# Loading a neighbourhood head's values: four copies of 32 rows in place of one copy over four groups of rows

## The chip, the cores and the metric

The kernel runs on one core of one Trainium2 chip. The metric is the device time of one execution in microseconds. The time before is the median of three runs; a profile of one further execution is read beside it. "PE" is the matrix engine, "DVE", "ACT" and "POOL" are the vector, scalar and general engines, and "SP" is the engine that here issues every DMA. A DMA copy is carried by up to 16 DMA engines side by side.

## What is computed

One layer of a hybrid trunk over 1024 latent tokens on a grid 64 wide (16 rows of 64) and 256 context tokens, all in float32: a half-step SwiGLU, then two token mixers on one normalised input (neighbourhood attention and latent attention, eight heads each), merged by gates, then a second half-step SwiGLU. The change lies in the neighbourhood attention. There, each block of 16 query columns reads keys and values from 32 neighbouring columns:

```
def row(r):
    rs = jnp.clip(r - kh // 2, 0, n_rows - kh)
    ...
    k_b = jnp.moveaxis(lax.dynamic_slice_in_dim(kg, rs, kh, axis=1)[:, :, key_col], 2, 1)
    v_b = jnp.moveaxis(lax.dynamic_slice_in_dim(vg, rs, kh, axis=1)[:, :, key_col], 2, 1)
    ...
    p = jax.nn.softmax(jnp.concatenate([s_loc, s_ctx], axis=-1), axis=-1).astype(v.dtype)
    o = (jnp.einsum('bhjqak,bjakhd->bjqhd', p_loc, v_b)
         + jnp.einsum('bhjqk,bkhd->bjqhd', p[..., n_loc:], v_ctx))
```

`key_col` gives, for column block j, the 32 columns from 0, 8, 24 or 32 on.

## The kernel before

The program runs in stages: first SwiGLU, the input projections, the attention stage, the merge, the second SwiGLU. The projections write queries, keys and values to DRAM scratch tensors (`qas`, `kas`, `vws` and others), and the attention stage reads them back head by head.

The attention stage works through a list `todo` of 64 items: items 0 to 31 are the eight neighbourhood heads with four column blocks each (`NaItem`, j = 0 to 3), items 32 to 63 are the eight latent-attention heads (`MlaItem`). An item has scores (matmuls into PSUM, the bias added on DVE, a softmax on ACT) and values (transposes, splits into a high and a low part, matmuls with the value tile, `weigh`). The scores of an item are computed three items ahead of its values (`AHEAD = 3`). `head_out` ends an item; its line 1777 runs once for each item and is used below as the mark of an item.

When the first item of a neighbourhood head is started, `NaHead.loads` issues all of that head's loads, in this order: `q` and `ql` (512 KB each), the context keys `kvc` (128 KB), the keys `k` (512 KB), the bias of block 0 (384 KB), the values `va` of blocks 0 and 1, the context values (128 KB), the bias of blocks 1 and 2, the values `vb` of blocks 2 and 3, the bias of block 3. A value tile (`va`, `vb`) holds two column blocks side by side, 512 KB. In `vws` a head's values are 256 rows of 512 floats: row r * 64 + x holds column x, and the four groups r are copied to partitions 32 r to 32 r + 31 of the tile. One column block is a quarter of the head's values, 256 KB, and is loaded by one call of `values`, which issued one DMA.

The weight tiles `W` come from a pool of 16 buffers, eight of which a head takes, so the loads of a head wait for tiles of earlier heads. `ld` goes through `put`, line 132, which issues on SP; every load and store in the program therefore has line 132. SP takes its DMAs in the order of the program. The framework gives the DMAs eight completion semaphores in turn (DMAHW0 to DMAHW7 in the rows below), so that each DMA waits until the one eight places before it has landed. PE's order in the attention stage is that of the program; instructions on DVE, ACT and POOL that are not pinned are ordered by the framework's scheduler.

Of the kernel before, what the change touches and what calls it, by code (L numbers as in the profile page):

```python
# [33 lines left out]
KSTART = (0, 8, 24, 32)  # L34
# [4 lines left out]
def f32(ap):  # L39
    return ap.bitcast(F32)  # L40
# [3 lines left out]
def hybrid_block(ctx: ExitStack, tc: tile.TileContext, a: dict, out: bass.AP):  # L44
# [37 lines left out]
    def DR(shape):  # L82
        n = nm("d")
        return dp.tile(shape, F32, tag=n, name=n)
# [37 lines left out]
    def ld(dst, src):  # L122
        for x in [x for x in waiting if x[1].tensor.name == src.tensor.name]:
            waiting.remove(x)
            put(*x[1:])
        return put(dst, src)
# [4 lines left out]
    def put(dst, src):  # L131
        return pin(nc.sync.dma_start(dst, src))  # L132
# [949 lines left out]
    o = len(plan.main)  # L1082
# [93 lines left out]
    o = d1_at + 4 * NP  # L1176
# [9 lines left out]
    for f, x in ups:  # L1186
        o = len(plan.main)
# [5 lines left out]
    for e in range(2):  # L1193
        for f in range(NF):
            o = len(plan.main)
# [70 lines left out]
    def emit_cq(i, ci, x, bank):  # L1266

        t, q = x, T2()
        if bank:
            t = T2()  # L1270
            act.copy(t, x)
        act.activation(q, t, AF.Square)
        if ci in sq:
            vec.tensor_tensor(sq[ci], sq[ci], q, op=ALU.add)
        else:
            sq[ci] = q
        store(cqx[i, :, ci * 512:(ci + 1) * 512], t)
# [22 lines left out]
    for p in range(3):  # L1300
        punits.append(Unit(h2, [cq_src(2 * p), cq_src(2 * p + 1)],
                           lambda i, ci, x, bank, p=p: emit_cq(2 * p + i, ci, x, bank)))

    o = len(plan.main)
# [46 lines left out]
    vws = DR([NH, 2 * P, 512])  # L1351
# [126 lines left out]
    o = len(plan.main)  # L1478
# [98 lines left out]
    class NaHead:  # L1577
# [46 lines left out]

        def values(self, v, j):
            o = (j % 2) * 512
            ld(f32(v[:, o:o + 512]), vws[self.h].rearrange("(r x) c -> r x c", r=4)[:, KSTART[j]:KSTART[j] + 32, :])

    def na_loads(h):
        heads["na", h] = x = NaHead()  # L1630
# [96 lines left out]
    o = c_at  # L1727
# [9 lines left out]
    o = len(plan.main)  # L1737
# [3 lines left out]
    o = len(plan.main)  # L1741
# [3 lines left out]
    o = len(plan.main)  # L1745
# [4 lines left out]
    o = len(plan.main)  # L1750
# [417 lines left out]
    for d in range(KD):  # L2168
        o = len(plan.main)
# [37 lines left out]
    o = len(plan.main)  # L2207
# [13 lines left out]
    o = len(plan.main)  # L2221
# [67 lines left out]
    for j in range(4):  # L2289
        o = d2_at + 5 * NP + 2 * j  # L2290
        for x, i in enumerate((-2, 0, 1)):
            plan.spread([lambda j=j, x=x: done2(j, x)], o + i, o + i + 1)
        o = e - 9 + j
        plan.spread([lambda j=j: done_half(4 + j, 1)], o, o + 1)
        o = e - 4 + j
# [83 lines left out]
```

## Time and profile before

| what | value |
|---|---|
| time before, median of 3 runs | 2599.38 us (2599.0 to 2601.32) |
| the profiled execution's own time | 2602.28 us |
| its span in the profile | 2600.5 us |
| mean granted clock of PE | 0.991 |
| PE busy | 2538.6 us, 98% |
| DVE busy | 1962.0 us, 75% |
| ACT busy | 1276.7 us, 49% |
| DMA | 471.74 MB, mean 181 GB/s |

Busy shares are means over stages that differ. The 40 slices of the page are 65 us each; the neighbourhood heads lie in slices 21 to 24, from about 1340 to 1535 us. A row of the windows view gives, for one stretch, each engine's busy time and instruction count, then PE's granted clock, the mean busy share of the 16 DMA engines, and the GB/s moved. Shares a little over 1 occur because packets overlap at their ends. A row of the view of one line gives the shortest, median and longest duration, and the first and last start. "SPq" is SP's DMA queue: its durations are those of issuing a DMA, not of its transfer.

### The profile page before, as it was taken

To read this page: it belongs to the slowest core of one execution; us is meant where nothing else is said; L and a number is where in the kernel's file an instruction comes from. 1 tells how busy PE (TensorE), PEld (TensorE's weight loads), DVE (VectorE), ACT (ScalarE), POOL (GpSimd) and SP (SyncE) were. 2 spreads that over 40 slices of the span, in tenths; PEclk is the share of its full clock that TensorE was granted. 3 is DMA by queue.
4 is the path that set the end of the run, shared out by engine and by line. 5 is a ranking of instruction groups with operands and counts; after the bars stand their busy time and mean duration, and the time that the engine had idled before them with its cause. 6 is when DMAs were issued, how large, how long until landed. Compare 5 with 4: busy or idle time off the path is not lost.

```text
span 2600.5 us, 38171 instructions
## 1 busy us (share of the span) xinstructions
PE 2538.6 (98%) x13368; PEld 2171.9 (84%) x13368; DVE 1962.0 (75%) x3671; ACT 1276.7 (49%) x2417; POOL 235.7 (9%) x388
## 2 busy tenths in 40 slices
PE   8999999999999999999988899999999999999998
PEld 6888888888998888889877789998888888888887
DVE  4788986797675578867756788887886888767777
ACT  6623224446654743435546777785167422333444
POOL 1000000001100000003003322221011000000003
PEclk9999999999999999999998999999999999999999
DMA  8555543943765556845866653214846444336824
GB/s 306 166 174 192 181 161 127 328 134 125 261 233 164 210 210 202 280 131 171 297 223 191 186 122 76 76 31 152 330 166 221 154 160 157 115 103 220 284 73 162
DMA packets 236289, 471.74 MB, mean 181 GB/s; under 512 B 30208, under 2 KB 63680, under 8 KB 236096
## 3 DMA queue, kind: packets, MB, share of 16 engines
q1 hardware_dynamic: 236096, 469.29, 54.3%
q8 instruction: 106, 1.74, 0.3%
q14 instruction: 87, 0.71, 0.1%
HBM read 348.80 MB, written 120.39 MB: 180 GB/s over the span
## 4 chain that ended last, share of the span: by engine, by line
PE 80%; DVE 6%; ACT 6%; DMA 5%; issue 3%; SPq 1%; POOL 0%; DVEq 0%; POOLq 0%; ACTq 0%
PE bs L154 34%; PE bm L154 25%; PE bv L154 18%; ACT xu L1936 2%; DVE xu L1800 2%; DMA w<-in_bias 1%; DVE t L1963 1%; ACT t L1962 1%; PE bm L157 1%; DMA xy<-in_bias 1%; DVE xu L120 1%; DVE xv L120 1%; ACT t L120 1%; SPq L132 1%; DMA w<-d 1%
## 5 line engine op out<-in xcount | busy, mean ns | idle before, releaser
L120 ACT CAST xu<-t 128x512 fp32r<-128x512 f32 (+1 forms) x270 | 160.9, 601 | 494.0 <-DVE t L120 352.4
L154 PE MATMUL bm<-xu,xu 128*128 128x512 f32 (+1 forms) x1500 | 356.6, 391 | 0.1
L154 PE MATMUL bs<-xv,xu 128*128 128x512 f32 (+1 forms) x1452 | 347.6, 388 | 0.6 <-DVE xv L120 0.3
L154 PE MATMUL bv<-xv,xu 128*128 128x512 f32 x1342 | 335.5, 389 | 0.0
L154 PEld LDWEIGHTS bm<-xu,xu 128*128 128x128 f32 x1500 | 278.2, 188 | 57.0 <-DVE t L120 0.5
L154 PEld LDWEIGHTS bs<-xv,xu 128*128 128x128 f32 x1452 | 272.0, 188 | 56.8 <-issue 1.1
L154 PEld LDWEIGHTS bv<-xv,xu 128*128 128x128 f32 x1342 | 251.8, 188 | 52.2
L154 PE MATMUL bs<-xv,xv 128*128 128x512 f32 (+1 forms) x1134 | 274.6, 387 | 0.0
L120 DVE TENSOR_TENSOR xu<-xu,xu 128x512 fp32r<-128x512 f32 (+2 forms) x300 | 203.9, 683 | 60.6 <-ACT xu L120 60.5
L154 PEld LDWEIGHTS bs<-xv,xv 128*128 128x128 f32 x1134 | 211.3, 188 | 40.8
L154 PE MATMUL bs<-w,w 96*128 96x512 f32 (+3 forms) x832 | 214.6, 377 | 28.7 <-DMA w<-d 15.1
L120 DVE TENSOR_TENSOR t<-t,t 128x512 f32<-128x512 f32 (+2 forms) x278 | 185.0, 672 | 43.2 <-ACT t L120 34.2
L154 PE MATMUL bs<-xu,xu 128*128 128x512 f32 x900 | 216.0, 388 | 0.0
L120 POOL TENSOR_SCALAR st<-st 128x1 f32<-128x1 f32 (+1 forms) x66 | 35.8, 542 | 1918.8 <-ACT t L120 1621.6
L154 PEld LDWEIGHTS bs<-xu,xu 128*128 128x128 f32 x900 | 167.7, 188 | 35.7 <-issue 1.4
L120 ACT CAST xv<-t 128x512 fp32r<-128x512 f32 x170 | 105.8, 622 | 166.1 <-PE bm L154 69.5
L120 DVE TENSOR_TENSOR xu<-t,xu 128x512 fp32r<-128x512 f32 (+1 forms) x270 | 179.0, 663 | 10.7 <-ACT xu L120 10.6
L154 PE MATMUL bm<-xv,xv 128*128 128x512 f32 (+1 forms) x690 | 182.7, 388 | 0.0
L120 ACT CAST xu<-xu 128x512 fp32r<-128x512 f32 (+1 forms) x226 | 133.7, 603 | 72.6 <-DMA xu<-in_wo 50.9
L120 DVE TENSOR_TENSOR xv<-t,xv 128x512 fp32r<-128x512 f32 x170 | 116.6, 686 | 65.3 <-ACT xv L120 64.9
L154 PEld LDWEIGHTS bs<-w,w 96*128 96x128 f32 (+1 forms) x832 | 128.9, 198 | 40.7 <-DVE st L1825 12.3
L154 PE MATMUL bv<-t,w 128*128 128x256 f32 x896 | 153.7, 293 | 7.5 <-issue 5.9
(250 smaller groups left out, 4352.0 us busy)
## 6 DMA issues: line engine op xcount, KB each, us to landing
d<-t SPq DMA_DIRECT2D x358, 256.0 KB, 2.5
t<-d SPq DMA_DIRECT2D x274, 256.0 KB, 3.8
xu<-in_f1w SPq DMA_DIRECT2D x59, 512.0 KB, 4.1
xu<-in_f2w SPq DMA_DIRECT2D x58, 512.0 KB, 3.6
t<-in_wada SPq DMA_DIRECT2D x112, 256.0 KB, 5.5
xv<-in_f1w SPq DMA_DIRECT2D x44, 512.0 KB, 8.2
xu<-in_winT SPq DMA_DIRECT2D x34, 512.0 KB, 4.8
w<-d SPq DMA_DIRECT2D x32, 512.0 KB, 13.9
```

The costliest lines, as they stand in the source:

```text
L120: return lambda *x, **y: pin(f(*x, **y))
L132: return pin(nc.sync.dma_start(dst, src))
L154: return pin(nc.tensor.matmul(o, s, m, start=start, stop=stop, skip_group_check=open_group[0]))
L157: return pin(nc.tensor.transpose(o, x, i))
L1800: nc.vector.tensor_scalar(dst, src, 1.0, FMIN, op0=ALU.mult, op1=ALU.max, accum_out=m)
L1936: nc.scalar.activation(x, x, AF.Exp, bias=n_[:, s:s + 1], accum_out=l[:, i:i + 1])
L1962: nc.scalar.copy(t[0], pb)
L1963: nc.vector.tensor_tensor(t[1], pb, f32(t[0]), op=ALU.subtract)
```

## The change

```diff
         def values(self, v, j):
             o = (j % 2) * 512
-            ld(f32(v[:, o:o + 512]), vws[self.h].rearrange("(r x) c -> r x c", r=4)[:, KSTART[j]:KSTART[j] + 32, :])
+            for r in range(4):
+                x = r * 64 + KSTART[j]
+                ld(f32(v[r * 32:r * 32 + 32, o:o + 512]), vws[self.h, x:x + 32, :])
```

The same bytes go to the same places. Each of the 32 loads of a column block's values becomes four loads of 64 KB, so the program issues 96 DMAs more. Lines after 1627 move down by two.

On SP, the loads of one head in the middle of the stage stand as follows before (`w_13386` and `w_13392` are the two value tiles, `d_368` is `vws`):

```order
L132 DMA w_13376<-d_360 128x1024
L132 DMA w_13377<-d_360 128x1024
L132 DMA w_13378<-d_364 128x256
L132 DMA w_13382<-d_364 128x1024
L132 DMA w_13384<-in_bias 128x768
L132 DMA w_13386<-d_368 128x1x512 x2
L132 DMA w_13378<-d_369 128x256
L132 DMA w_13390<-in_bias 128x768
L132 DMA w_13392<-d_368 128x1x512 x2
L132 DMA xy_13395<-in_bias 128x768
```

and now, for the same head:

```order
L132 DMA w_13400<-d_360 128x1024
L132 DMA w_13401<-d_360 128x1024
L132 DMA w_13402<-d_364 128x256
L132 DMA w_13406<-d_364 128x1024
L132 DMA w_13408<-in_bias 128x768
L132 DMA w_13410<-d_368 32x512 x8
L132 DMA w_13402<-d_369 128x256
L132 DMA w_13420<-in_bias 128x768
L132 DMA w_13422<-d_368 32x512 x8
L132 DMA xy_13431<-in_bias 128x768
```

The order of the tiles is the same; a head's 12 DMAs have become 24.

Where the attention stage begins, SP's queue has the last stores of the projections (`d_374`) ahead of the loads for heads 0 and 1. Before:

```order
L132 DMA d_374<-t_12990 128x512
L132 DMA d_374<-t_12991 128x512
L132 DMA xu_13044<-in_bias 128x768
L132 DMA w_13046<-d_368 128x1x512 x2
L132 DMA w_13096<-in_bias 128x768
L132 DMA w_13119<-d_368 128x1x512 x2
L132 DMA w_12883<-d_369 128x256
L132 DMA w_13123<-d_368 128x1x512 x2
L132 DMA xy_13126<-in_bias 128x768
```

and now:

```order
L132 DMA xu_13050<-in_bias 128x768
L132 DMA d_374<-t_12996 128x512
L132 DMA d_374<-t_12997 128x512
L132 DMA w_13052<-d_368 32x512 x8
L132 DMA w_13108<-in_bias 128x768
L132 DMA w_13131<-d_368 32x512 x8
L132 DMA w_12889<-d_369 128x256
L132 DMA w_13141<-d_368 32x512 x8
L132 DMA xy_13150<-in_bias 128x768
```

One bias load has moved ahead of two stores, and three pairs of value loads have become three groups of eight.

PE's order does not change. On DVE the scheduler places some unpinned instructions otherwise, with the same instructions in total. At the start of the stage, before (1825 and 1800 are scores, 1832 and 1838 the softmax's maximum and reciprocal, 1859 a low part):

```order
L1825 ISA w_12859,st_12860<-bs_12869,w_12742 128x384
L1825 ISA st_12860 128x1
L1800 TENSOR_SCALAR w_12859,st_12860<-bs_12857 128x256
L1838 RECIPROCAL st_12805<-st_12804 128x2
L1859 TENSOR_TENSOR t_12890<-bv_12891,t_12889 128x512
L1832 TENSOR_REDUCE st_12861<-st_12860 128x2
```

and now (the same lines, two higher):

```order
L1827 ISA w_12865,st_12866<-bs_12875,w_12748 128x384
L1827 ISA st_12866 128x1
L1802 TENSOR_SCALAR w_12865,st_12866<-bs_12863 128x256
L1834 TENSOR_REDUCE st_12867<-st_12866 128x2
L1840 RECIPROCAL st_12811<-st_12810 128x2
L120 TENSOR_TENSOR t_12850<-t_12848,t_12849 128x512
```

The maximum of item 1 now stands ahead of the reciprocal of item 0 and ahead of a split of the projections (line 120).

## The prediction

> **What bounds the kernel now.** I read the page's slices first, then the chain that ended last, then the windows of the stage with the change, then SP's issues.
>
> ```profile
> span 2600.5 us, 38171 instructions
> PE 2538.6 (98%) x13368; PEld 2171.9 (84%) x13368; DVE 1962.0 (75%) x3671; ACT 1276.7 (49%) x2417; POOL 235.7 (9%) x388
> ...
> PE   8999999999999999999988899999999999999998
> ...
> PEclk9999999999999999999998999999999999999999
> ```
>
> PE is the bound over the whole, except in slices 21 to 23, the neighbourhood heads: there it falls to 8 tenths and its clock dips. The chain in that stretch shows what stands in PE's place (start us, us, what):
>
> ```profile
> 1358.16 15.63 DMA xy<-in_bias
> 1375.79 11.12 DMA w<-in_bias
> 1406.71 14.03 DMA w<-d
> ...
> 1444.38 14.79 DMA xy<-in_bias
> 1461.49 11.56 DMA w<-in_bias
> 1482.89 12.45 DMA w<-in_bias
> 1504.76 5.57 DMA w<-d
> ```
>
> Seven transfers make 85 us of chain. They are late, not large: a bias is 384 KB. Three stretches inside this stage, a stretch of four latent-head items, one just before the stage and one with copies of fewer rows show the DMA side (the last three columns are PE's clock, the DMA share, GB/s):
>
> ```profile
> 1376.20:1515.10 138.90, 114.88 (x776) 110.12 (x777) 97.27 (x352) 95.35 (x225) 50.69 (x87) 0.88 0.67 187
> 1530.00:1560.00 30.00, 30.00 (x219) 28.09 (x218) 26.34 (x81) 25.00 (x58) 8.23 (x14) 1.00 0.33 82
> 1379.00:1382.00 3.00, 3.00 (x15) 3.00 (x14) 1.09 (x3) 1.15 (x2) 0.00 (x0) 0.50 0.26 96
> 1392.30:1396.30 4.00, 4.00 (x34) 3.94 (x32) 3.66 (x14) 3.94 (x10) 2.13 (x4) 1.00 0.27 104
> 1384.00:1391.40 7.40, 7.21 (x58) 7.01 (x57) 5.92 (x20) 6.16 (x15) 3.61 (x7) 1.00 1.04 270
> 1331.30:1337.00 5.70, 5.70 (x35) 5.01 (x34) 4.64 (x15) 2.73 (x5) 0.00 (x0) 1.00 0.74 282
> 1564.00:1568.50 4.50, 4.50 (x33) 4.10 (x32) 3.84 (x14) 3.80 (x9) 0.29 (x1) 1.00 0.52 130
> ```
>
> The transfers alternate between two states: stretches with a share of 1.04 at 270 GB/s, and stretches with a share of 0.26 or 0.27 at about 100 GB/s. A share of 0.26 over 16 engines is four engines busy and twelve idle. SP's issues tell whose they are (shortest/median/longest ns, first to last start):
>
> ```profile
> L132 SPq DMA_DIRECT2D w<-d x70: 308/537/3200, 1376.4 to 1514.8; - x70
> ...
> L132 SPq DMA_DIRECT2D w<-in_bias x11: 333/483/619, 1375.8 to 1482.9; - x11
> L132 SPq DMA_DIRECT2D xy<-in_bias x6: 2253/2340/2428, 1379.7 to 1487.7; - x6
> ```
>
> The two bias rows are the same kind of copy, yet the one issued right behind the value loads (`xy`) takes 2.3 us to issue and the other 0.48 us, and some `w<-d` take 3.2 us: something behind the value loads is full. So I read the value loads, whose source has an outer dimension of 4, as confined to four engines. Then those four carry far more than the rest. The sizes are on the page:
>
> ```profile
> w<-d SPq DMA_DIRECT2D x32, 512.0 KB, 13.9
> w<-d SPq DMA_DIRECT2D x64, 256.0 KB, 3.7
> ...
> w<-in_bias SPq DMA_DIRECT2D x16, 384.0 KB, 14.0
> ```
>
> A head loads 3 x 512 + 2 x 128 + 3 x 384 = 2944 KB that all engines share, 184 KB each, and 4 x 256 = 1024 KB of values, 256 KB on each of four. Those four move 440 KB in a head. At a quarter of 100 GB/s, 25 KB/us, that is 17.6 us with nothing else running, and more when all 16 run, where each has 270 / 16 = 17 KB/us. A head takes:
>
> ```profile
> L1777 DVE TENSOR_TENSOR t<-t,bv x26: 406/418/425, 1376.2 to 1515.1; 64x256 f32<-64x256 f32 x26
> ```
>
> 26 items end from 1376.2 to 1515.1, so 25 steps take 138.9 us, 5.56 us each, 22.2 us for a head of four. Four overloaded engines explain that length.
>
> [...]
>
> **The change part by part.**
>
> Spreading the values. The four engines no longer carry more than the others; a head's load is 3968 KB over 16. What comes next is one of three.
>
> First, the items themselves. Inside a head, where no load is awaited, three items run in a row:
>
> ```profile
> L1777 DVE TENSOR_TENSOR t<-t,bv x3: 425/425/425, 1389.4 to 1397.7; 64x256 f32<-64x256 f32 x3
> ...
> L1777 DVE TENSOR_TENSOR t<-t,bv x3: 407/407/408, 1410.2 to 1418.9; 64x256 f32<-64x256 f32 x3
> ...
> L1777 DVE TENSOR_TENSOR t<-t,bv x3: 425/425/425, 1432.5 to 1440.8; 64x256 f32<-64x256 f32 x3
> ...
> L1777 DVE TENSOR_TENSOR t<-t,bv x3: 407/408/408, 1453.3 to 1461.5; 64x256 f32<-64x256 f32 x3
> ```
>
> Two steps take 8.3, 8.7, 8.3 and 8.2 us, mean 8.4, so 4.2 us an item and 16.8 us a head.
>
> Second, the DMA engines. 2944 KB are 3.01 MB, at 270 GB/s 11.2 us. The values, 1.05 MB, go at some rate between 130 GB/s (the row from 1564.00, copies of 64 and 32 rows for the latent heads, partly idle) and 270 GB/s: 8.1 to 3.9 us. I take 6.0, the middle, since neither row is nearer in kind. Sum 17.2 us, ends 15.1 and 19.3.
>
> Third, SP. It issues 24 DMAs a head in place of 12. No row shows a load of 32 rows by 2 KB. The nearest rows are the latent heads' loads of 64 and 32 rows (median 580 ns) and stores of 32 rows (median 1024 ns):
>
> ```profile
> L132 SPq DMA_DIRECT2D w<-d x94: 303/580/1594, 1509.9 to 1705.4; - x94
> ...
> L132 SPq DMA_DIRECT2D d<-t x2: 939/1024/1108, 1272.6 to 1273.8; - x2
> ```
>
> I take 580 ns, a load like these. 16 x 0.58 + 8 x 0.48 = 13.1 us a head, below the other two. The waits for a DMA eight places back stay, but the DMA eight back now lands sooner; what queues behind SP is only the next loads, and DVE and PE wait for those as they do now.
>
> The largest is 17.2 us. I add 0.6 us because three resources lie within 4 us of each other and won't overlap perfectly: 17.8 us a head. The gain is 22.2 - 17.8 = 4.4 us on each of 25 / 4 = 6.25 heads, 27.5 us. Ends: with the values at 130 GB/s 19.3 + 0.6 = 19.9 and a gain of 14 us; with items at 4.0 us, since part of these runs was at half clock, and nothing else in the way, 16.0 and 39 us.
>
> Where the stage begins. Here DVE and PE wait for the same kind of transfer (us in all, times, longest):
>
> ```profile
> DVE xu L1825 <- DMA w<-in_bias: 20.2, 8, 5.4
> PE bs L154 <- DMA w<-d: 15.1, 9, 4.3
> ...
> DVE xu L1825 <- DMA xy<-in_bias: 5.6, 3, 3.5
> ```
>
> Of these, the waits ahead of 1376.2 are one for `w<-in_bias` (5.4) and one for `xy<-in_bias` (3.5). But SP has three groups of eight value loads before that `xy` bias, 24 x 0.6 = 14 us, where six value loads were issued between 1347.0 and the bias at 1358.16:
>
> ```profile
> L132 SPq DMA_DIRECT2D w<-d x80: 308/537/3596, 1347.0 to 1509.9; - x80
> ```
>
> So it is issued some 4 us later, and lands within an estimated 5 us (384 KB and the value copies ahead of it at 270 GB/s) instead of 15.63. I count 2 us of gain; ends 0 and 6.
>
> The moves on DVE swap neighbouring instructions. They cost nothing where the bias is awaited anyway, and at most one wait of 1 to 2 us either way where the projections end, with PE still at work there. Taken at 0. Before the stage, six more issues for head 0's first value tile, 6 x 0.58 = 3.5 us of SP, lie under a PE that is busy throughout (5.70 of 5.70 us from 1331.30); without that cover they would cost up to 3.5 us.
>
> After the stage PE is the bound again (30.00 of 30.00 us from 1530.00), so what is saved stays saved. The sum: 2602.28, the profiled execution's own time, less 27.5 and 2, is 2572.8. That execution was 2.9 us above the median of 2599.38, so the forecast is 2570 us.
>
> **The rivals.**
>
> The narrow copies stay slow. 32 rows may not be able to take in what 16 engines bring: the row from 1564.00, at half share and 130 GB/s with 64- and 32-row copies, speaks for it; that SP has little to issue there speaks against. It gives 19.9 us a head, a gain of 14 us, 2585 us. [...]
>
> SP becomes the bound, and the kernel is slower. If an issue of 32 rows costs 1.1 us, as in the longest of the two stores, a head needs 16 x 1.1 + 8 x 0.48 = 21.4 us, with about 0.05 us between issues (24 x 0.05 = 1.2) 22.6 us, 0.4 more than now, 2.5 us in all; and at the stage's begin 24 issues are 26 us where 11 were, some 15 us later with 11 won back on the landing, 4 us. It gives 2606 us. It decides from 1.07 us an issue: (22.2 - 1.2 - 3.8) / 16. For it: stores of 32 rows do take that long. Against: 94 loads have a median of 580 ns.
>
> The change does nothing. If the value loads are on 16 engines already and slow for the DRAM tensor they read, four copies take as long as one: 2599 us. Against it is the share of 0.26, and the row from 1331.30, where stores and loads of scratch tensors run at 282 GB/s.
>
> **How the numbers follow.** Forecast 0.64; narrow copies 0.20; SP 0.10; nothing 0.06. The range takes in the first two with their ends: from 2554 (gain 39 and 6 on 2599.4) to 2590 (the narrow copies with nothing won at the begin and 5 us of issue gaps). Left out are the 0.16 of the last two. Faster by over 0.2% (5.2 us, about what a measurement of this kernel can tell from no change): 0.64 + 0.20 = 0.84. Within: 0.06. Slower: 0.10.
>
> **What would show it.** The stretches with a share of 0.26 at 100 GB/s are gone; the `xy` bias is issued in under 0.7 us; the transfers of 11 to 15 us in the chain are under 8; line 1777's (now 1779) 25 steps take about 111 us rather than 138.9; SP's value loads have a median near 0.58 us; PE's clock in the stage rises above 0.88. Wrong would be: value loads that take over 1 us to issue with SP busy throughout the stage, or stretches at a quarter share still there.

## The result, and the profile after

The changed kernel takes 2582.3 us (median of four runs, 2581.56 to 2583.79) where the kernel before takes 2599.2 in the same comparison. The ratio is 0.9934, with a 95% interval from 0.9917 to 0.9951. That is a gain of 16.9 us; 29.4 us had been forecast. The profiled execution after took 2582.79 us.

The page after, its head and the slices of PE and of PE's granted clock:

```profile
span 2581.0 us, 38289 instructions
...
PE   8999999999999999999998899999999999999998
...
PEclk9999999999999999999999999999999999999999
```

Slice 21 is back at 9 tenths and no slice's clock is under 9 tenths any more, but two slices of the neighbourhood heads still stand at 8. DMA issues of the page and the one long transfer that is left in the chain between 1344 and 1520 us (issues: KB each, median us to landing; chain: start us, us, what):

```profile
w<-d SPq DMA_DIRECT2D x32, 512.0 KB, 5.8
w<-d SPq DMA_DIRECT2D x144, 64.0 KB, 2.7
...
w<-in_bias SPq DMA_DIRECT2D x16, 384.0 KB, 4.5
...
1363.94 5.86 DMA w<-d
```

A bias now lands after 4.5 us in place of 14.0, and of the seven transfers of 5.57 to 15.63 us in the chain before, one of 5.86 is left. The stage's long window, three stretches with value loads in it, and SP's issues from 1376 to 1515 us (columns as before):

```profile
1376.20:1515.10 138.90, 120.26 (x848) 113.13 (x847) 108.97 (x385) 102.37 (x245) 54.15 (x92) 0.95 0.64 193
1366.50:1369.50 3.00, 0.73 (x5) 0.30 (x2) 2.82 (x11) 0.89 (x2) 1.83 (x3) 1.00 1.04 369
1383.00:1386.00 3.00, 3.00 (x20) 3.00 (x19) 2.20 (x10) 0.98 (x4) 0.00 (x0) 0.67 1.03 356
1402.00:1403.00 1.00, 1.00 (x8) 1.00 (x6) 0.42 (x2) 1.00 (x3) 0.00 (x0) 0.53 1.06 249
```

```profile
L132 SPq DMA_DIRECT2D w<-d x143: 302/419/1114, 1375.9 to 1514.4; - x143
...
L132 SPq DMA_DIRECT2D xy<-in_bias x6: 422/423/424, 1376.8 to 1471.0; - x6
```

The first two stretches are mixed: of their 369 and 356 GB/s, packets of 2 KB, the rows of the values, make only 29 and 71, and the rest is mostly rows of queries, keys and bias. In the third, 240 of the 249 GB/s are rows of the values, at a share of 1.06, where the stretch from 1379.00 before moved 96 GB/s of them at 0.26. So the value loads now use all 16 engines. SP issues a bias behind them in 0.42 us, where it took 2.34. So the loads did what they were meant to do. The time is not where the forecast put it, though. The marks of the items, before and after (the fourth to the 28th mark, then the 28th to the 32nd):

```profile
L1777 DVE TENSOR_TENSOR t<-t,bv x25: 406/411/425, 1376.2 to 1506.3; 64x256 f32<-64x256 f32 x25
L1777 DVE TENSOR_TENSOR t<-t,bv x5: 407/424/425, 1506.3 to 1535.5; 64x256 f32<-64x256 f32 x5
```

```profile
L1779 DVE TENSOR_TENSOR t<-t,bv x25: 402/415/425, 1366.4 to 1493.1; 64x256 f32<-64x256 f32 x25
L1779 DVE TENSOR_TENSOR t<-t,bv x5: 407/424/425, 1493.1 to 1515.7; 64x256 f32<-64x256 f32 x5
```

The fourth mark comes 9.8 us earlier (1376.2 to 1366.4). The 24 steps behind it take 126.7 us in place of 130.1, only 3.4 us less, and the last four 22.6 in place of 29.2, which is 6.6 less. The sum, 19.8 us, is close to the difference of the spans (19.5, which is more than the 16.9 of the medians because the profiled execution before was itself 2.9 us above its median). The 24 steps, where some 26 us were expected, gave almost nothing. The waits from 1376 to 1500 us after the change say what stands there now (us in all, times, longest):

```profile
PEld bs L154 <- DVE st L1827: 22.8, 22, 2.5
ACT xu L1836 <- DVE st L1834: 22.5, 17, 2.6
PE bs L154 <- DVE st L1827: 18.3, 15, 2.3
```

PE does not wait for any transfer in this window. It waits for line 1827, the bias addition on DVE, and ACT waits for line 1834, the maximum on DVE. The timeline of DVE where one head gives way to the next, with PE's burst that follows (start us, us, instruction, in brackets the idle time before it and what ended it):

```profile
1398.14 0.69 DVE L1861 TENSOR_TENSOR t<-bm,t 128x512 fp32r<-128x512 f32 x1 [0.78 <-ACT t L1860]
1398.74 0.40 DVE L1779 TENSOR_TENSOR t<-t,bv 64x256 f32<-64x256 f32 x1
1399.07 0.41 DVE L1861 TENSOR_TENSOR xu<-bm,xu 128x256 fp32r<-128x256 f32 x1
1399.50 0.69 DVE L1861 TENSOR_TENSOR t<-bm,t 128x512 fp32r<-128x512 f32 x1
1400.11 0.55 DVE L1827 CUSTOM_DVE_ANT_0 xu<-bs,w 128x384 f32<-128x384 f32 x1
...
1400.72 1.10 PE L154 MATMUL bs<-w,w 128*128 128x256 f32 x4 [1.87 <-DVE st L1827]
```

DVE waits 0.78 us for a high part of the old head and does the low parts (1861) and the end of an item (1779), and only then the bias additions of the next head's second item (1827); those of its first item came earlier. PE sits idle for 1.87 us, and behind that its granted clock stands at 0.50:

```profile
1402.10:1405.50 3.40, 3.40 (x17) 3.40 (x16) 1.92 (x9) 1.81 (x5) 0.00 (x0) 0.50 0.53 127
```

For 3.4 us PE is busy throughout, at that clock. The step from the mark at 1398.7 to the next one takes 8.5 us; those that follow it inside the head take 3.7 to 4.8. The scheduler's order is what the added DMAs changed here, on DVE and, less, on ACT and POOL, and the experiments below test whether it is the cause. DVE's order around the boundary between two heads, at the bias additions of the new head's second item (its bias tile is `w_13689` before and `w_13731` now), before:

```
L1825 ISA xu_13770,st_13772<-bs_13775,w_13689 128x384
L1825 ISA st_13772 128x1
L1859 TENSOR_TENSOR t_13786<-bm_13787,t_13785 128x512
L1825 ISA xu_13771,st_13772<-bs_13795,w_13689 128x384
L1825 ISA st_13772 128x1
L1800 TENSOR_SCALAR xu_13770,st_13772<-bs_13769 128x256
...
L1777 TENSOR_TENSOR t_13808<-t_13808,bv_13754 64x256
```

and now:

```
L1861 TENSOR_TENSOR t_13834<-bm_13835,t_13833 128x512
L1779 TENSOR_TENSOR t_13856<-t_13856,bv_13802 64x256
L1861 TENSOR_TENSOR xu_13061<-bm_13862,xu_13061 128x2x128
L1861 TENSOR_TENSOR t_13874<-bm_13875,t_13873 128x512
L1827 ISA xu_13818,st_13820<-bs_13823,w_13731 128x384
L1827 ISA st_13820 128x1
L1827 ISA xu_13819,st_13820<-bs_13843,w_13731 128x384
```

Before, a low part stood between the two bias additions and the end of the old head's item behind them. Now three low parts and that end stand ahead of both.

### The profile page after: what moved, and what is told of

Same layout as the page of the kernel before. It is cut to its first block, busy times and chain, and to the rows that moved or that the text cites. A ratio compares the mean times of both kernels' runs of the same rounds, so it can differ in the third digit from the quotient of the medians.

```text
span 2581.0 us, 38289 instructions
## 1 busy us (share of the span) xinstructions
PE 2532.1 (98%) x13368; PEld 2165.3 (84%) x13368; DVE 1963.8 (76%) x3671; ACT 1276.3 (49%) x2417; POOL 232.3 (9%) x388
## 4 chain that ended last, share of the span: by engine, by line
PE 82%; ACT 7%; DVE 7%; issue 3%; DMA 1%; SPq 0%; POOL 0%; DVEq 0%; POOLq 0%; ACTq 0%
PE bs L154 35%; PE bm L154 26%; PE bv L154 19%; PE bm L157 2%; DVE xu L1802 2%; ACT xu L1938 1%; DVE t L1965 1%; ACT t L1964 1%; DVE xu L120 1%; ACT xu L1836 1%; DVE xv L120 1%; PE bs L157 1%; ACT t L120 1%; DVE t L120 1%; ACT t L1860 1%
## 5 line engine op out<-in xcount | busy, mean ns | idle before, releaser
L154 PE MATMUL bm<-t,xu 128*128 128x256 f32 (+1 forms) x1252 | 156.8, 286 | 0.0
```

Source lines behind the costliest of these rows:

```text
L154: return pin(nc.tensor.matmul(o, s, m, start=start, stop=stop, skip_group_check=open_group[0]))
```

## The experiments

The theory (A): the four copies free the four DMA engines and are worth some 30 us by themselves, and the new order on DVE takes some 17 of that back. The main rival (B): the head is bound by something that comes with narrow copies, SP's issues or the intake of 32 rows, and the order on DVE only shows it.

**The order pinned, with the new and the old loads.** In both kernels four DVE instructions of a neighbourhood item that the scheduler could move (bias addition, maximum, reciprocal, low part) are pinned to the program's order. The copy of the context's scores with its maximum (line 1800) and the end of an item (1777) stay unpinned. Pinned instructions are recorded at line 120.

```diff
-                nc.vector.tensor_tensor_reduce(out=pr[s][:, :384], in0=loc[:, :384],
+                vec.tensor_tensor_reduce(out=pr[s][:, :384], in0=loc[:, :384],
...
-            nc.vector.tensor_reduce(n_, ...)
+            vec.tensor_reduce(n_, ...)
...
-                nc.vector.reciprocal(r, l)
+                vec.reciprocal(r, l)
...
-                nc.vector.tensor_tensor(ol, src, f32(oh), op=ALU.subtract)
+                vec.tensor_tensor(ol, src, f32(oh), op=ALU.subtract)
```

With the four copies:

> Four copies of 32 rows, and the DVE instructions of a neighbourhood item that add the bias, take the maximum, invert the sum and make the low part are kept in the order of the program. Theory A (the loads no longer pace the changed kernel; what is left between two heads is the scheduler's order on DVE, which puts the bias add of the next head's first item behind three low parts): the long step of about 8 us in each head shrinks to about 5, 20.4 us a head become about 17.5, time about 2565 us. Theory B (the narrow copies or SP's issues still pace the heads): no change, about 2582 us.

With the one copy of before. The orders are then nearly those of the kernel above. PE's is the same; 26 of some 3400 instructions on DVE stand elsewhere (19 of them copies of line 1800), 21 of some 2150 on ACT and one on POOL:

> One copy over four groups as before, with the same DVE instructions kept in the order of the program; its DVE order is then the same as that of the kernel with four copies. Theory A (four DMA engines pace the heads whatever the order on DVE): about 2597 us, within 4 us of before, and the stretches at a quarter of the DMA share stay. Theory C (the change acted through the DVE order that the scheduler made of it, and not through the loads): the time falls to 2582 us or below.

Measured: 2561.14 us with the four copies, ratio 0.9844 (0.9829 to 0.9858), and 2598.75 us with the one, ratio 0.9992 (0.9982 to 1.0002), beside 2600.69 for the kernel before. At one order of the pinned instructions the loads are worth 37.6 us. With the new loads the order is worth 21 us (2582.3 to 2561.1, from two comparisons). With the old loads the pins bring 2 us at the medians, and the interval takes in no change at all. That pair does not price the changed kernel's order under the old loads, because from the third head on the order before already had the bias additions of each second item where the pins put them. The marks, four copies first, then one:

```profile
L1779 DVE TENSOR_TENSOR t<-t,bv x25: 407/409/427, 1367.4 to 1471.4; 64x256 f32<-64x256 f32 x25
```

```profile
L1777 DVE TENSOR_TENSOR t<-t,bv x25: 407/414/425, 1375.6 to 1505.5; 64x256 f32<-64x256 f32 x25
```

The 24 steps take 104.0 us against 129.9: a gain of 25.9, at an order that is nearly the same. Of the 37.7 us between the spans, 8.2 lie before the fourth mark and the remaining 3.6 behind the 28th. The waits and the windows of the pinned kernel with four copies show the cover that is back:

```profile
ACT xu L1836 <- DVE st L120: 7.0, 14, 1.0
...
PE bs L154 <- DVE st L120: 3.9, 9, 0.6
```

```profile
1344.00:1376.00 32.00, 25.89 (x174) 23.68 (x173) 22.69 (x87) 20.07 (x49) 8.49 (x15) 0.95 0.68 215
1376.00:1500.00 124.00, 119.96 (x912) 115.19 (x911) 114.72 (x407) 109.68 (x259) 57.24 (x98) 1.00 0.75 224
```

PE's waits for DVE fell from 18.3 us to 3.9 and the longest from 2.3 to 0.6; its clock is 1.00 and it is busy for 119.96 of 124 us. The 14.4 us of waits, and the 6.9 us that a clock of 0.95 in place of 1.00 makes over the 138.9 us of the long window, come to about the 21 us, as an estimate. So the loads gain more than A says, and the scheduler's order was what kept 21 us of it. The pins are on DVE alone, but behind them the scheduler places some 35 instructions of ACT and 15 of POOL otherwise too; that it is DVE's part that costs the time is read from PE's waits for lines 1827 and 120 and was not tried by itself.

**Two copies and eight.** If the number of engines decides, two copies that each run over two groups should be far worse than one copy over four, and eight copies of 16 rows as good as four unless SP's issues are the price. Both have the pins. Two copies:

```diff
-            for r in range(4):
-                x = r * 64 + KSTART[j]
-                ld(f32(v[r * 32:r * 32 + 32, o:o + 512]), vws[self.h, x:x + 32, :])
+            rows = vws[self.h].rearrange("(r x) c -> r x c", r=4)[:, KSTART[j]:KSTART[j] + 32, :]
+            for r in range(2):
+                ld(f32(v[r * 64:r * 64 + 64, o:o + 512]), rows[2 * r:2 * r + 2])
```

> Two copies, each over two groups of 32 rows, same DVE pins. Theory A (a copy runs on as many engines as its outer dimension allows, here 2): a head puts 184 + 512 = 696 KB on two engines, at 25 KB/us 28 us in place of 22, so about 40 us slower than before, about 2640 us, with stretches at a DMA share of 0.13. Rival (the size or the number of copies in flight decides, not the outer dimension): between the one copy and the four copies, 2570 to 2597 us.

Eight:

```diff
-                x = r * 64 + KSTART[j]
-                ld(f32(v[r * 32:r * 32 + 32, o:o + 512]), vws[self.h, x:x + 32, :])
+                for y in range(2):
+                    x = r * 64 + KSTART[j] + y * 16
+                    p = r * 32 + y * 16
+                    ld(f32(v[p:p + 16, o:o + 512]), vws[self.h, x:x + 16, :])
```

> Eight copies of 16 rows, same DVE pins; each still has an outer dimension of 16. Theory A (all 16 engines are used, and 32 more issues of 0.42 us a head, 17 us with the rest, still fit under a head): within 5 us of four copies with pins. Theory B (narrow copies are slow, or SP's issues pace): over 10 us slower than four copies with pins, since both costs double.

Two copies took 2678.43 us, ratio 1.0298 (1.0283 to 1.0314). A stretch of its value loads, the issue of the bias behind them, and the marks:

```profile
1403.00:1411.00 8.00, 2.73 (x23) 2.50 (x21) 1.41 (x6) 3.37 (x8) 1.84 (x4) 0.93 0.13 48
```

```profile
L132 SPq DMA_DIRECT2D xy<-in_bias x4: 2577/2581/2622, 1377.7 to 1473.5; - x4
```

```profile
L1779 DVE TENSOR_TENSOR t<-t,bv x25: 404/414/425, 1394.8 to 1584.7; 64x256 f32<-64x256 f32 x25
```

A share of 0.13 is two engines of 16, and 48 GB/s are half of the 96 that the stretch at 0.26 moved before. The direction and the number of engines are as A has them. The size is not: 80 us lost beside the one pinned copy, where 40 were expected. A head takes 189.9 / 6 = 31.7 us. I had 28, reckoned from two engines with nothing else running. Of the 80 us, 60 lie in the 24 steps and 19 ahead of the fourth mark (1375.6 to 1394.8), which the expectation did not count.

Eight copies took 2616.25 us, ratio 1.0057 (1.0042 to 1.0072), 55 us more than four. A missed this. A stretch of the value loads, and SP's issues in it:

```profile
1389.00:1394.00 5.00, 4.43 (x34) 4.22 (x35) 4.91 (x18) 3.14 (x9) 1.86 (x3) 1.00 0.29 69
```

```profile
L132 SPq DMA_DIRECT2D w<-d x9: 414/418/418, 1388.7 to 1392.4; - x9
```

Eight gaps in 3.7 us are 0.46 us from one issue to the next. 32,768 bytes in each are 71 GB/s, which is what the stretch moves. So SP sets the rate of the values there. PE's scores (`bs`) wait, for queries and keys that SP issues behind the values:

```profile
PE bs L154 <- DMA w<-d: 32.2, 12, 9.5
```

The 24 steps take 140.9 us, 23.5 us a head. In them SP issues 240 DMAs, which takes 105.3 us and some 11 us between them. What remains is SP's own waiting, mostly for earlier loads (us in all, times, longest):

```profile
SPq L132 <- DMA w<-d: 17.1, 13, 2.1
SPq L132 <- DMA w<-in_bias: 5.9, 6, 1.4
```

So with eight copies SP issues or waits throughout.

An issue takes 0.418 us for 16 rows, and 0.419 was the median in the changed kernel with its 32. With 16 rows the issue is not slower than with 32; there are more issues. B is right on SP at eight copies, not at four.

**Both column blocks in one copy.** If SP's issues are the price and the number of rows is not, a copy that takes 32 rows of both column blocks should be as good as two, at half the issues.

```diff
-            for j in range(2):
-                self.values(va, j)
+            self.values(va, 0)
...
-                ld(f32(v[r * 32:r * 32 + 32, o:o + 512]), vws[self.h, x:x + 32, :])
+                ap = vws[self.h, x:x + 40, :]
+                src = bass.AP(tensor=ap.tensor, offset=ap.offset, ap=[[512, 32], [8 * 512, 2], [1, 512]])
+                ld(f32(v[r * 32:r * 32 + 32, :]).rearrange("p (b c) -> p b c", b=2), src)
```

With the scheduler's order, which on DVE, ACT and POOL is that of the changed kernel, and with the pins, where it is that of the pinned four copies:

> Both column blocks of a value tile in one copy for each group of 32 rows (32 rows by 2 by 2 KB): eight value loads a head in place of sixteen, the same bytes, DVE as the scheduler orders it, which is the order of the changed kernel. Theory A (that order on DVE paces the changed kernel's heads, not the loads): within 6 us of 2582 us. Theory B (SP's issues pace it): SP has 3.7 us less to issue in each head, about 20 us less, 2562 us.

> The same loads, and the DVE pins of the four copies with pins. Theory A: from 1376 us on PE is already busy for 97% with four copies and pins, so what fewer issues can win is at the stage's begin, where PE idles for 6 us of 32 and waits for loads that SP has yet to issue: 2 to 6 us less than 2561 us, about 2557 us. Rival (SP's issues don't matter with four copies either): the same as 2561 us within 2 us.

Measured: 2578.82 us, ratio 0.9913 (0.9898 to 0.9928), and with the pins 2557.73 us, ratio 0.9828 (0.9812 to 0.9845), beside 2601.85 before. The pins are worth 21.1 us here, as they were with four copies a block. The second is the best version of all. SP's issues and the marks of it:

```profile
L132 SPq DMA_DIRECT2D w<-d x104: 302/428/1544, 1376.6 to 1497.8; - x104
```

```profile
L1778 DVE TENSOR_TENSOR t<-t,bv x25: 407/409/425, 1368.7 to 1468.4; 64x256 f32<-64x256 f32 x25
```

An issue of 32 x 2 rows costs 0.43 us. The 24 steps fall from 104.0 to 99.7 us, but all of the difference lies in the first of them, 8.6 us against 4.3. Behind it both kernels take 4.15 us an item, about the pace of the items within a head before (4.2). So fewer issues win something where the stage begins, as expected, and nothing in the heads that follow.

**Four copies, but all on four engines.** This kernel has as many copies and bytes as the changed one, but each runs over all four groups and takes a quarter of the columns. If it is the number of DMAs that helps, it should gain; if it is the engines, it should not.

```diff
-            for r in range(4):
-                x = r * 64 + KSTART[j]
-                ld(f32(v[r * 32:r * 32 + 32, o:o + 512]), vws[self.h, x:x + 32, :])
+            rows = vws[self.h].rearrange("(r x) c -> r x c", r=4)[:, KSTART[j]:KSTART[j] + 32, :]
+            for c in range(0, 512, 128):
+                ld(f32(v[:, o + c:o + c + 128]), rows[:, :, c:c + 128])
```

> Four copies for each column block again, but each over all four groups of 32 rows and a quarter of the 512 columns, so with an outer dimension of 4 and rows of 512 B in place of 2 KB; as many DMAs as in the changed kernel, and the scheduler makes a changed DVE order of them. Theory A (a copy over four groups stays on four engines, so four copies of that kind bring nothing): not faster than before, 2600 us or, with the shorter rows, up to 2625 us, with stretches at a DMA share of 0.26. Rival (more and smaller copies in flight are what helped): faster than before, 2575 to 2590 us.

With the pins:

> The same loads with the DVE pins. Theory A: the loads pace the heads, so the pins bring at most 5 us against the same loads without them, 2595 to 2620 us. Rival (the DVE order is worth 20 us whatever the loads do): about 20 us less than without pins.

Measured: 2609.75 us, ratio 1.0031 (1.0019 to 1.0044), and 2608.02 us with the pins, ratio 1.0027 (1.0015 to 1.0039), beside 2601.71 before. A stretch of value loads without the pins:

```profile
1390.80:1393.50 2.70, 2.08 (x15) 1.90 (x15) 2.61 (x12) 1.24 (x3) 0.73 (x1) 1.00 0.30 75
```

The share of 0.30 is near the 0.26 and 0.27 of the old loads, and nothing is gained: the kernel is 8 us slower than before. The pins are worth 1.7 us here, and the two intervals overlap. The scheduler's order of this kernel is not that of the changed one (one low part more, not three and an end, stands ahead of a second item's bias additions), so this does not price that order either. The pinned kernel is the closest partner of the pinned four copies: as many copies, the same bytes, and an order that differs in 7 instructions on DVE and one on ACT, at 2608.02 us against 2561.14. Its rows are shorter, 512 bytes in place of 2 KB, and the stretch above moved 75 GB/s where the one from 1379.00 before moved 96; what the shorter rows cost by themselves was not separated. It is the spreading, and not the number of copies, that makes the gain.

## Why the prediction was right or wrong

| kernel | copies for a block | 24 steps, us | time, us |
|---|---|---|---|
| before | 1 | 130.1 | 2599.2 |
| changed | 4 | 126.7 | 2582.3 |
| old loads, pinned | 1 | 129.9 | 2598.75 |
| changed, pinned | 4 | 104.0 | 2561.14 |
| both blocks in one, pinned | 2 (4 for two) | 99.7 | 2557.73 |

The direction was right and the time lies within the range, but the forecast of 2570 us is between two kernels, the changed one and the pinned one, and for neither of them is it right. That the time lies within the range is in part luck: the loads gave more than was forecast, the order took some 21 us back, and the range reached up to 2590 us for narrow copies, which did not come.

- **The four engines.** Right. The stretches at a share of 0.26 and 0.27 give way to one of 1.06 after the change, with two copies a stretch stands at 0.13, and with four copies that each run over four groups one stands at 0.30. In the stretch from 1379.00 before, all of the 96 GB/s are packets of 2 KB, the rows of the values. The forecast spread a head's 3968 KB over 16 engines; no run showed then that the new copies would use all of them, and the share of 1.06, with 240 GB/s of rows of the values, is what the changed kernel showed in its place.
- **The saving on 24 steps.** 4.4 us on each of six heads, 26.4 us, was expected, and 25.9 us were measured at one order of the pinned instructions. The working behind it was less right than the sum. Of the three limits, the items (16.8 us a head) are what is left, not the DMA (17.2): behind the first step a pinned head takes 4 x 4.15 = 16.6 us, with sixteen value loads or with eight. That is 5.0 us less than the 21.6 (129.9 / 6) of the old loads, and the first step, 8.6 us, hid some of it. The 4.0 us an item of the range's fast end leaned on half clock in part of the runs of three items, which the trace does not show: PE's granted clock is 1.00 in all four of them. The values moved 240 GB/s in the stretch from 1402.00, near the upper end of the 130 to 270 that I bounded them by, where I took 6.0 us, or 175 GB/s. SP's issue is 0.42 us and not 0.58.
- **"The moves on DVE swap neighbouring instructions. They cost nothing where the bias is awaited anyway".** This is the step that failed. It was taken at 0, and at most 1 to 2 us; it cost 21. I read the orders where the stage begins, and there they do swap neighbours. At each boundary of two heads the new order puts three of the old head's low parts and the end of an item ahead of the bias additions of the new head's second item (not of its first, as the expectation for the pins has it), and that comes back with every head from the third on. My reason, that the bias is awaited there anyway, leans on late transfers, and those are what the change removes: after it, PE waits for no transfer there from 1376 to 1500 us. Whether the late transfers of the old loads would have covered this order is not shown, since no run has the two together. The orders of ACT and POOL, which I did not look at, moved too.
- **The begin of the stage.** Mis-sized: 2 us (0 to 6) expected, 9.8 us measured, 8.2 with the pins on both sides. With the pins, 7.7 of the 8.2 lie in the three steps up to the fourth mark; without them, 5.8 of the 9.8. I set the later issue of the bias against its faster landing, and SP's issues, at 0.42 us and not 0.58, make that lateness smaller; what else the begin gained from was not separated.
- **The end of the stage.** It was not a term of its own; the forecast had 1.1 us for its part of the steps beyond the 24th. The last four steps gave 6.6 us with the changed order, and with the pins all that lies behind the 28th mark gave 3.6.
- **The sum.** 26.4 + 2 + 1.1 = 29.5 was expected. The loads alone gave 25.9 + 8.2 + 3.6 = 37.7 in the spans, and the order took some 21 back, nearly all of it from the 24 steps (104.0 to 126.7).
- **The rivals.** The narrow copies do not stay slow. The stretch from 1402.00, with many copies of 32 rows in it, moved 240 GB/s of their rows, where the forecast's row for this rival had 130 at half share. No run has one such copy alone. SP as the bound comes true with eight copies, through the number of issues and at 0.42 us each, where I had 1.07 us as the point from which it decides. That the change does nothing is excluded by the pinned pair and by the changed kernel itself.

Open: why the scheduler orders DVE otherwise when there are more DMAs was not tried, nor the changed kernel's order with the old loads, nor one narrow copy alone.

## What to carry to other kernels

Copies with an outer dimension of 4 ran at a DMA share of 0.26 here, and with one of 2 at 0.13: look for stretches at such a share, and for long issues of the copies behind them (2.34 us here, 0.42 after). After an edit that only touches loads, compare the order of the waiting engines at the boundary that repeats, not only where the stage begins, and cost the difference against the kernel as it will be, because a late transfer that might have covered an order may be on time by then. When a gain comes out too small, hold the order and change the loads, then the other way round: two runs separated 37.6 us of loads from 21 us of order here.

## What the runs showed of the hardware

- SP's issue of a copy took 0.42 us for 16 rows, 0.42 for 32 and 0.43 for 32 x 2. At 0.46 us from one to the next, copies of 32 KB from one queue come to 71 GB/s, and a stretch of them moved 69.
- Copies over four groups moved 96 GB/s at a DMA share of 0.26 with rows of 2 KB, and 75 at 0.30 with rows of 512 bytes; copies over two groups moved 48 at 0.13. Copies of 32 rows moved 240 of the 249 GB/s of a stretch at 1.06.
- A wait of 1.87 us on PE was followed by 3.4 us at a granted clock of 0.50. The step in which both lie takes 8.5 us; with the pins, where PE's longest wait for DVE from 1376 to 1500 us is 0.6 us and the clock there is 1.00, the steps behind the first take 3.7 to 4.6.
